# Moving and weight operands of the fp32r matmuls placed at fixed offsets by padding the on-chip pools

## The chip, the cores and the metric

The kernel runs on one core of a Trainium2 chip. The metric is the device time of one execution in microseconds (us). The kernel before took 1050.9 us (median of three runs, 1048.54 to 1056.88).

## The reference, cut to what matters

Two transformer blocks are applied to one sequence of 256 tokens with 1024 features, all in fp32:

- Block one: `x += 0.5*g*swiglu(h)` (hidden width 2816), then a mixer (latent attention with 8 heads beside a short convolution, merged by sigmoid gates and an output projection), then a second swiglu. Each `h` is an RMS norm of `x`, scaled and shifted by vectors that a 1024 x 9216 matrix makes from a condition vector `c`.
- Block two: a mixer of two attentions with gates, a feed-forward `square(relu(h @ w_ff1)) @ w_ff2` (hidden width 4096), a gated addition, and a final RMS norm.

Nearly all of the work is in products of a 256-token activation with weight matrices of 1024 rows or 1024 columns. None of the values computed differ between the two kernels.

## The kernel before

**Three products per tile.** Every fp32 weight tile `raw` that arrives by DMA is split by `split` (L130 to L141) into two fp32r tiles, `hi` (ScalarE, L139) and `lo` (VectorE, L140), and every activation likewise (`hilo`, L171). `mm3` (L149) then issues three matmuls into one PSUM region: `hi` with the high activation, `hi` with the low one, `lo` with the high one:

```
pe.matmul(ps, lhsT=wh, rhs=xh, ...)   # L150
pe.matmul(ps, lhsT=wh, rhs=xl, ...)   # L151
pe.matmul(ps, lhsT=wl, rhs=xh, ...)   # L152
```

`lhsT` is the stationary operand (the weights, 128 x 128, loaded by a LDWEIGHTS), `rhs` is the moving one (128 x 256 tokens). From the loops there are 7,536 fp32r matmuls of 256 columns, and 84 of 384 to 512. In 420 of the 7,620 (latent projection, the heads of both mixers, `natural`) `mm3n` (L166) turns the roles around: there the activation is stationary and the weight tile moves.

**Stages.** In order: the start (condition vector, first norm); swiglu one; mixer one; swiglu two; mixer two; the feed-forward of block two; the gated end. In a swiglu (`swiglu`, `stream_ffn`, 11 iterations) `make` computes 96 matmuls of gate and up strips into the tiles `gu`, and `second` 48 matmuls of the down projection into four accumulators `acc0` to `acc3`, one iteration behind. The feed-forward of block two does the same in 16 iterations, with 48 matmuls into `u` and 48 into `acc`. Other products are in `gl`, `y`, `po` (mixer one) and `qa`, `qkb`, `ya`, `gab`, `po` (mixer two). SyncE issues the weight DMAs; each engine works in program order, and TensorE is fed by the splits of ScalarE and VectorE that run ahead of it.

**Where tiles lie.** In each partition the pools lie one after the other (`const`, `wp`, `tmp`, `res`, then the pools of a stage: `mp` in the streamed feed-forwards, `px` in the mixers), each tile after the one before it, rounded up to 32 bytes. So the size of what comes earlier sets the offset of what follows. In bytes modulo 128, the kernel before has:

| tiles | pool | offset mod 128 |
|---|---|---|
| `hh`, `hl` (activation of most products), `pH`, `pL` | `res` | 0 |
| `mh`, `ml` (activation of the down projections) | `mp` | 0 |
| `ocH`, `ocL`, `mg`, `oAH`, `oAL`, `oBH`, `oBL` | `px` | 0 |
| `oaH`, `oaL`, and `cqH`, `cqL`, `ckH`, `ckL` | `px` of mixer one | 64 |
| `hi`, `lo` of all strips outside the down projections | `wp` | 96 |
| `hi`, `lo` of swiglu one's down projection (`at=(8, 8)`) | `mp`, 2 buffers | 32 and 32, then 96 and 96 |
| the same, swiglu two (`at=(4, 12)`) | `mp` | 16 and 48, then 80 and 112 |
| the same, feed-forward of block two (`at=(8, 4)`) | `mp` | 32 and 16, then 96 and 80 |
| `ident`, `ones1024`, `sq` (moving, plain fp32) | `const`, `tmp` | 32 |

`at` is a pair of offsets in fp32 elements (4 bytes) inside tiles that are 16 elements longer than the 2048 needed; because of these 64 bytes the second of the two buffers lies 64 bytes further on modulo 128. Within a tile, the pieces that matmuls read start at multiples of 512 bytes, so an offset holds for all of them.

Of the kernel before, what the change touches and what calls it, by code (L numbers as in the profile page):

```python
# [8 lines left out]
F32 = mybir.dt.float32  # L9
# [9 lines left out]
P = 128  # L19
# [42 lines left out]
def tile_two_blocks(ctx: ExitStack, tc: tile.TileContext, t: dict, out: bass.AP):  # L62
# [3 lines left out]
    const = ctx.enter_context(tc.tile_pool(name="const", bufs=1))  # L66
    wp = ctx.enter_context(tc.tile_pool(name="wp", bufs=3))
    tmp = ctx.enter_context(tc.tile_pool(name="tmp", bufs=2))
    res = ctx.enter_context(tc.tile_pool(name="res", bufs=1))
# [4 lines left out]
    def bankA(name):  # L74
        return psA.tile([P, 512], F32, tag="acc", name=name)
# [23 lines left out]

    start = tc.tile_pool(name="start", bufs=1)  # L100
    start_ctx, start = start, start.__enter__()
    c_raw = const.tile([P, 8], F32, name="c_raw")
    sync.dma_start(out=c_raw, in_=t["c"][0].rearrange("(p k) -> p k", k=8))
    x_nat = start.tile([P, 2048], F32, name="x_nat")
# [24 lines left out]

    def split(raw, kc, n, wp=wp, bufs=3, at=None):  # L130

        pad = 16 if at else 0
        hi, lo = (wp.tile([P, 2048 + pad], F32R, tag=n_, name=n_, bufs=bufs)[:, o:o + 2048]
                  for n_, o in zip(("hi", "lo"), at or (0, 0)))
        tot = kc * n
        step = tot // pieces[0]
        for s in range(0, tot, step):
            sl = slice(s, s + step)
            act.copy(hi[:, sl], raw[:, sl])  # L139
            vec.tensor_tensor(out=lo[:, sl], in0=raw[:, sl], in1=hi[:, sl].bitcast(F32), op=ALU.subtract)  # L140
        return tuple(z[:, :tot].rearrange("p (k n) -> p k n", k=kc) for z in (hi, lo))  # L141
# [7 lines left out]
    def mm3(ps, wh, wl, xh, xl, start, stop):  # L149
        pe.matmul(ps, lhsT=wh, rhs=xh, start=start, stop=False, skip_group_check=True)  # L150
        pe.matmul(ps, lhsT=wh, rhs=xl, start=False, stop=False, skip_group_check=True)  # L151
        pe.matmul(ps, lhsT=wl, rhs=xh, start=False, stop=stop, skip_group_check=True)  # L152
# [127 lines left out]
    def ada_one(s, which, i):  # L280
        yield from ada_four(s * 24 + which * 8 + i)
        if which == 1:
            ada_scale(s, i, 4)
        if which == 2:
            vec.tensor_scalar_mul(gT[:, s * 8 + i:s * 8 + i + 4], modT[:, s * 24 + 16 + i:s * 24 + 20 + i],
                                  1.0 if s == 1 else 0.5)

    def ada_rest(plan, per, lag=1):

        todo = [ada_one(*a) for a in plan]  # L290
        begun = [[] for _ in range(lag)]
        step = 0
        while todo or any(begun):
            for g in begun.pop(0):
                next(g, None)
            n = per[step % len(per)]
            step += 1
            begun.append(todo[:n])
            todo = todo[n:]
            for g in begun[-1]:  # L300
                next(g)
            yield

    ada_plan = [(s, which, i) for s in range(3) for which in range(3) for i in (0, 4)][4:]

    def drain(g):
        for _ in g:
            pass
# [73 lines left out]
    def stream_ffn(nit, make, w2, finish, extra=None, at=None):  # L382
        with tc.tile_pool(name="mp", bufs=2) as mp:
            ada_tile[:] = [(lambda: mp.tile([P, 2048], F32, tag="ada", name="ada", bufs=2), 4)]
            acc = [bankA(f"acc{i}") for i in range(4)]

            def second(i, mh, ml, w):
                for q in range(4):
                    for d in (2 * q, 2 * q + 1):
                        ps = acc[q][:, (d % 2) * T:(d % 2) * T + T]  # L390
                        for j in range(2):
                            mm3(ps, w[0][:, j, d * P:(d + 1) * P], w[1][:, j, d * P:(d + 1) * P], mh[:, j, :], ml[:, j, :],
                                i == 0 and j == 0 and d % 2 == 0, i == nit - 1 and j == 1)
                    if i == nit - 1:
                        for d in (2 * q, 2 * q + 1):
                            finish(d, acc[q][:, (d % 2) * T:(d % 2) * T + T])

            prev = None
            for i in range(nit):
                mh = mp.tile([P, 2, T], F32R, tag="mh", name="mh")  # L400
                ml = mp.tile([P, 2, T], F32R, tag="ml", name="ml")
                make(i, mh, ml, mp)
                if prev is not None:
                    second(*prev)
                prev = (i, mh, ml, cols(w2, 0, D, 2 * i, 2, at=at, wp=mp, bufs=2))
                if extra is not None:
                    next(extra, None)
            if extra is not None:
                drain(extra)
            second(*prev)  # L410
# [13 lines left out]
    def swiglu(h, w13, w2, gcol, extra=None, fill=None, then=(), first=None, at=None):  # L424
        def make(i, mh, ml, mp):
            if i == 0 and first:
                bb = first
            else:
                g, u = up_strips(w13, i)
                bb = [bankB("gu") for _ in range(2)]  # L430
            if i == 0 and fill is not None:
                fill()
            if i == 0 and not first:
                gemm_many([(b[:, o:o + T], w, j * P) for j, b in enumerate(bb) for o, w in ((0, g), (T, u))], h, KD)
            for j, b in enumerate(bb):
                if i:
                    gemm(b[:, :T], g, j * P, h, KD)
                    gemm(b[:, T:], u, j * P, h, KD)
                s = tmp.tile([P, T], F32, tag="s", name="s")
                m = tmp.tile([P, T], F32, tag="m", name="m")  # L440
                tab(s, b[:, :T], AF.Silu)
                vec.tensor_tensor(out=m, in0=s, in1=b[:, T:], op=ALU.mult)
                hilo(m, mh[:, j, :], ml[:, j, :])
            if i < len(then):
                then[i]()
        stream_ffn(11, make, w2, residual(gcol), extra, at)
# [13 lines left out]
    gt = lambda s: gT[:, s * 8:s * 8 + 8]  # L460
# [82 lines left out]
    h = h_tiles()  # L543

    h = h_tiles()
    rope_steps = rope_table()
# [5 lines left out]
    first = [bankB("gu") for _ in range(2)]  # L552
# [15 lines left out]
    def gemm_half(i):  # L568
# [13 lines left out]
    start_ctx.__exit__(None, None, None)  # L582
    swiglu(h, t["ffn_w13"][0][0], t["ffn_w2"][0][0], gt(0), ada_rest(ada_plan[:8], (0, 0, 1, 1, 1, 1, 1, 1, 1, 1)),
           then=(lambda: None, vector_columns, transpose_p, lambda: next(rope_steps), lambda: None,
                 lambda: drain(rope_steps)), first=first, at=(8, 8))
    mid = ada_rest(ada_plan[8:12], (1,))


    def mixer_one(px, tmp2):
        h = modulated(nw(1), sh(1))  # L590
# [35 lines left out]
        def latent():  # L626
# [19 lines left out]
            for tk in range(2):  # L646
# [2 lines left out]
                vec.tensor_scalar_mul(kr[:, tk, :], bb[tk][:, 384:416], r[:, 3 * tk + 2:3 * tk + 3])  # L649
                rope(kro[:, tk:tk + 1, :], kr[:, tk:tk + 1, :], 1, tk, 1)  # L650
            yield
            cqH = px.tile([P, 2, T], F32R, tag="oaH", name="cqH")
            cqL = px.tile([P, 2, T], F32R, tag="oaL", name="cqL")
            ckH = px.tile([P, T], F32R, name="ckH")
# [254 lines left out]
        return bt  # L909

    h = modulated(nw(2), sh(2))
    swiglu(h, t["ffn_w13"][0][1], t["ffn_w2"][0][1], gt(2), ada_rest(ada_plan[12:], (1,)), fill=bias_rows, at=(4, 12))


    def mixer_two(px, tmp2):
# [290 lines left out]
    h, make_rb = gained("mlp")  # L1206
    rbs = []

    def make(i, mh, ml, mp):
        w = cols(t["w_ff1_2"][0], i * 256, 256)  # L1210
        b = bankB("u")
        for j in range(2):
            gemm(b[:, j * T:(j + 1) * T], w, j * P, h, KD)
        if i == 0:
            rbs.append(make_rb())
        s = mp.tile([P, 2, T], F32, tag="s2", name="s")
        m = mp.tile([P, 2, T], F32, tag="m2", name="m")
        vec.scalar_tensor_tensor(out=s, in0=halves(b), scalar=0.0, in1=rbs[0].unsqueeze(1).to_broadcast([P, 2, T]),
                                 op0=ALU.max, op1=ALU.mult)
        act.activation(m, s, AF.Square)  # L1220
        hilo(m, mh, ml)

    stream_ffn(16, make, t["w_ff2_2"][0], add_x, at=(8, 4))


    with tc.tile_pool(name="px3", bufs=1) as px:
# [4 lines left out]
        h, make_rb = gained("ple")  # L1231
# [7 lines left out]
        def finish(part, c0, n, banks):  # L1239

            for tk in range(2):
                for i in range(n):
                    tr(banks[tk][:, i * P:(i + 1) * P], xT[:, c0 + i, tk * P:(tk + 1) * P])
                fin[part, tk] = banks[tk][:, :n * P]
            for tk in range(2):
                junk = px.tile([P, 512], F32, tag="junk", name="junk", bufs=2)
                act.activation(junk[:, :n * P], fin[part, tk], AF.Square, accum_out=s2[:, tk, part:part + 1])
                sl = slice(c0 * P, (c0 + n) * P)
                if part < 2:
                    vec.tensor_tensor(out=fg[tk][:, sl], in0=fin[part, tk], in1=gbc[:, sl], op=ALU.mult)  # L1250
# [104 lines left out]
```

## Time and profile before

| | |
|---|---|
| time of three runs | 1056.88, 1050.9, 1048.54 us; median 1050.9 us |
| time of the profiled execution | 1048.57 us |
| its span, first to last instruction | 1046.8 us |
| mean granted TensorE clock | 0.995 |
| busy: PE, VectorE, ScalarE, GpSimd | 97%, 71%, 53%, 3% |
| chain of waits: PE, VectorE, ScalarE, DMA | 82%, 9%, 3%, 3% |

Each matmul is recorded with a duration of about 280 ns, which overlaps the next matmuls. What a matmul costs in a dense stream is the distance from its start to the start of the next one; this text calls that a slot. It is read from two rows of the time-ordered list: the last start of a block less the first, divided by the matmuls between them.

### The profile page before, as it was taken

How to read it: one execution, taken by the hardware profiler on the slowest of the kernel's cores; microseconds unless marked ns; L12 is line 12 of the kernel's file. 1: busy time of each engine (PE TensorE's matmuls, PEld its weight loads, DVE VectorE, ACT ScalarE, POOL GpSimd, SP SyncE). 2: the span in 40 equal slices, each digit the busy share in tenths (PEclk: the TensorE clock that was granted, in tenths of full speed). 3: DMA queues.
4: the chain of work that ended last, by engine and by line, in shares of the span. 5: the costliest groups of instructions: out<-in, count | busy, mean ns of one | idle time of the engine just before them, and what ended most of it. 6: DMA issues, size and time to landing. Idle time of an engine off the chain costs nothing.

```text
span 1046.8 us, 20303 instructions
## 1 busy us (share of the span) xinstructions
PE 1018.4 (97%) x8332; PEld 984.3 (94%) x8332; DVE 741.7 (71%) x1414; ACT 557.3 (53%) x1036; POOL 34.9 (3%) x47
## 2 busy tenths in 40 slices
PE   6999999999999999999999999999999999999996
PEld 3799999999989998999999999999899999999996
DVE  4789998657967998964545689656467776555565
ACT  5564554447656455643444555544456665445453
POOL 0000000010000011000000100001100100000010
PEclk9999999999999999999999999999999999999998
DMA  9899999425754987986554344445335885555311
GB/s 346 287 373 337 304 343 367 142 87 173 214 178 151 290 262 271 343 274 212 170 193 153 112 128 155 135 135 165 96 123 188 267 285 186 183 187 195 121 62 41
DMA packets 161301, 215.41 MB, mean 206 GB/s; under 512 B 6206, under 2 KB 129877, under 8 KB 161080
## 3 DMA queue, kind: packets, MB, share of 16 engines
q1 hardware_dynamic: 159346, 212.58, 61.4%
q10 hardware_dynamic: 1862, 1.53, 0.5%
q8 instruction: 65, 1.06, 0.4%
q14 instruction: 28, 0.23, 0.1%
HBM read 210.63 MB, written 3.47 MB: 205 GB/s over the span
## 4 chain that ended last, share of the span: by engine, by line
PE 82%; DVE 9%; ACT 3%; DMA 3%; issue 1%; POOL 0%; SPq 0%; DVEq 0%; ACTq 0%; POOLq 0%
PE gu L150 8%; PE gu L152 8%; PE gu L151 8%; PE acc L150 7%; PE acc L151 7%; PE acc L152 6%; DVE lo L140 3%; PE u L152 2%; PE u L150 2%; PE u L151 2%; PE gab L150 1%; DMA ada<-in_w_ada_dram 1%; ACT hi L139 1%; PE gab L152 1%; PE gab L151 1%
## 5 line engine op out<-in xcount | busy, mean ns | idle before, releaser
L140 DVE TENSOR_TENSOR lo<-raw,hi 128x512 fp32r<-128x512 f32 (+2 forms) x454 | 395.7, 903 | 102.9 <-ACT hi L139 101.7
L139 ACT CAST hi<-raw 128x512 fp32r<-128x512 f32 (+2 forms) x454 | 337.1, 786 | 222.3 <-PE acc L151 81.6
L150 PE MATMUL gu<-hh,hi 128*128 128x256 f32 x704 | 198.8, 283 | 0.0
L152 PE MATMUL gu<-hh,lo 128*128 128x256 f32 x704 | 197.6, 281 | 0.0
L151 PE MATMUL gu<-hl,hi 128*128 128x256 f32 x704 | 196.8, 280 | 0.0
L150 PE MATMUL acc<-mh,hi 128*128 128x256 f32 x608 | 170.2, 282 | 2.3 <-ACT mh L172 2.3
L151 PE MATMUL acc<-ml,hi 128*128 128x256 f32 x608 | 170.8, 281 | 0.0
L152 PE MATMUL acc<-mh,lo 128*128 128x256 f32 x608 | 170.2, 280 | 0.0
L151 PEld LDWEIGHTS gu<-hl,hi 128*128 128x128 f32 x704 | 133.0, 189 | 0.6 <-issue 0.5
L150 PEld LDWEIGHTS gu<-hh,hi 128*128 128x128 f32 x704 | 132.9, 189 | 0.6 <-issue 0.5
L152 PEld LDWEIGHTS gu<-hh,lo 128*128 128x128 f32 x704 | 132.8, 189 | 0.1
L150 PEld LDWEIGHTS acc<-mh,hi 128*128 128x128 f32 x608 | 114.0, 188 | 2.8 <-ACT mh L172 2.8
L151 PEld LDWEIGHTS acc<-ml,hi 128*128 128x128 f32 x608 | 114.5, 188 | 0.2 <-DVE ml L173 0.2
L152 PEld LDWEIGHTS acc<-mh,lo 128*128 128x128 f32 x608 | 114.7, 189 | 0.0
L267 DVE SCALAR_TENSOR_TENSOR ada_acc<-ada,c_act,ada_acc 128x512 f32<-128x512 f32 x98 | 73.6, 751 | 2.3 <-DMA ada<-in_w_ada_dram 0.6
L150 PE MATMUL u<-hh,hi 128*128 128x256 f32 x256 | 71.6, 280 | 0.0
L151 PE MATMUL u<-hl,hi 128*128 128x256 f32 x256 | 71.6, 280 | 0.0
L152 PE MATMUL u<-hh,lo 128*128 128x256 f32 x256 | 71.5, 279 | 0.0
L88 ACT ACTIVATE s<-gu 128x256 f32<-128x256 f32 x44 | 16.7, 382 | 75.2 <-PE gu L152 75.2
L331 POOL TENSOR_TENSOR ssum<-ssum,sq 128x256 f32<-128x256 f32 x25 | 23.3, 931 | 813.6 <-ACT sq L329 812.6
L151 PEld LDWEIGHTS u<-hl,hi 128*128 128x128 f32 x256 | 48.1, 188 | 0.2 <-DVE hl L376 0.2
L150 PEld LDWEIGHTS u<-hh,hi 128*128 128x128 f32 x256 | 48.1, 188 | 0.0
(379 smaller groups left out, 2221.9 us busy)
## 6 DMA issues: line engine op xcount, KB each, us to landing
raw<-in_ffn_w_dram SPq DMA_DIRECT2D x64, 1024.0 KB
raw<-in_w_in_dram SPq DMA_DIRECT2D x37, 1024.0 KB
raw<-in_w_ff_dram SPq DMA_DIRECT2D x32, 1024.0 KB
ada<-in_w_ada_dram SPq DMA_DIRECT2D x28, 1024.0 KB
raw<-in_w_out_dram SPq DMA_DIRECT2D x8, 1024.0 KB
ada<-in_w_ada_dram SPq DMA_DIRECT2D x8, 768.0 KB
raw<-in_w_branch_dram SPq DMA_DIRECT2D x8, 512.0 KB
raw<-in_w_out_a_dram SPq DMA_DIRECT2D x4, 1024.0 KB
```

Source lines behind the costliest of these rows:

```text
L88: last_table[0] = act.activation(*args, **kw).ins
L139: act.copy(hi[:, sl], raw[:, sl])
L140: vec.tensor_tensor(out=lo[:, sl], in0=raw[:, sl], in1=hi[:, sl].bitcast(F32), op=ALU.subtract)
L150: pe.matmul(ps, lhsT=wh, rhs=xh, start=start, stop=False, skip_group_check=True)
L151: pe.matmul(ps, lhsT=wh, rhs=xl, start=False, stop=False, skip_group_check=True)
L152: pe.matmul(ps, lhsT=wl, rhs=xh, start=False, stop=stop, skip_group_check=True)
L267: vec.scalar_tensor_tensor(out=acc, in0=wv[:, k, :], scalar=c_act[:, k0 + k:k0 + k + 1], in1=acc, op0=ALU.mult, op1=ALU.add)
L331: pool.tensor_tensor(out=s[0], in0=s[0], in1=sq, op=ALU.add)
```

## The change

Unused tiles are put into three pools, and the two offsets of the streamed feed-forwards are made equal everywhere.

- `pad_w`, 24 fp32 elements (96 bytes) at the head of `const`, moves everything behind it by 96 bytes: `wp` goes from 96 to 64 modulo 128, `ident`, `ones1024` and `sq` from 32 to 0.
- `pad_x`, 8 elements (32 bytes) at the head of `res`, moves `res` and the stage pools by 128 bytes in all, so their tiles stay at 0.
- `pad_o`, 16 elements (64 bytes) in `px` of mixer one, moves what is created after it: `cqH`, `cqL`, `ckH`, `ckL`, `oaH`, `oaL` from 64 to 0.
- In `split`, tiles with an `at` become 32 elements longer (128 bytes) instead of 16, and all three `at` become (16, 16): `hi` and `lo` of the down projections lie at 64 modulo 128 in both buffers.

No instruction is added, removed or reordered.

```
+    const.tile([P, 24], F32, name="pad_w")
+    res.tile([P, 8], F32, name="pad_x")
     c_raw = const.tile([P, 8], F32, name="c_raw")
...
-        pad = 16 if at else 0
+        pad = 32 if at else 0
...
-                 lambda: drain(rope_steps)), first=first, at=(8, 8))
+                 lambda: drain(rope_steps)), first=first, at=(16, 16))
...
+            px.tile([P, 16], F32, name="pad_o")
             cqH = px.tile([P, 2, T], F32R, tag="oaH", name="cqH")
...
-    swiglu(h, ..., fill=bias_rows, at=(4, 12))
+    swiglu(h, ..., fill=bias_rows, at=(16, 16))
...
-    stream_ffn(16, make, t["w_ff2_2"][0], add_x, at=(8, 4))
+    stream_ffn(16, make, t["w_ff2_2"][0], add_x, at=(16, 16))
```

## Rows read from the trace of the kernel before

**Rows 1.** The page, busy time: busy us, share of the span, instructions

```profile
PE 1018.4 (97%) x8332; PEld 984.3 (94%) x8332; DVE 741.7 (71%) x1414; ACT 557.3 (53%) x1036; POOL 34.9 (3%) x47
```

**Rows 2.** Stretches: length; busy per engine; granted clock; DMA share; GB/s

```profile
35.90:225.50 189.60, 189.60 (x1676) 188.77 (x1675) 159.32 (x250) 100.01 (x147) 2.26 (x4) 1.00 0.84 287
```

**Rows 3.** The page, costliest groups: line, operation, count, busy us, mean ns

```profile
L150 PE MATMUL gu<-hh,hi 128*128 128x256 f32 x704 | 198.8, 283 | 0.0
...
L150 PE MATMUL acc<-mh,hi 128*128 128x256 f32 x608 | 170.2, 282 | 2.3 <-ACT mh L172 2.3
...
L150 PE MATMUL u<-hh,hi 128*128 128x256 f32 x256 | 71.6, 280 | 0.0
```

**Rows 4.** List in order of time: start us, duration us; a `gu` block, 95 slots

```profile
80.78 0.28 PE L150 MATMUL gu<-hh,hi 128*128 128x256 f32 x1
...
91.86 0.28 PE L152 MATMUL gu<-hh,lo 128*128 128x256 f32 x1
```

**Rows 5.** The same list, a later `gu` block from its second matmul, 94 slots

```profile
98.17 0.28 PE L151 MATMUL gu<-hl,hi 128*128 128x256 f32 x1
...
109.24 0.28 PE L152 MATMUL gu<-hh,lo 128*128 128x256 f32 x1
```

**Rows 6.** The same list, down projection of swiglu one, 47 slots

```profile
91.98 0.28 PE L150 MATMUL acc<-mh,hi 128*128 128x256 f32 x1
...
97.54 0.28 PE L152 MATMUL acc<-mh,lo 128*128 128x256 f32 x1
```

**Rows 7.** The same list, swiglu two, both buffers, 47 slots each

```profile
500.39 0.28 PE L150 MATMUL acc<-mh,hi 128*128 128x256 f32 x1
...
505.92 0.28 PE L152 MATMUL acc<-mh,lo 128*128 128x256 f32 x1
...
517.25 0.28 PE L150 MATMUL acc<-mh,hi 128*128 128x256 f32 x1
...
522.79 0.28 PE L152 MATMUL acc<-mh,lo 128*128 128x256 f32 x1
```

**Rows 8.** The same list, feed-forward of block two, both buffers, 47 slots each

```profile
863.24 0.28 PE L150 MATMUL acc<-mh,hi 128*128 128x256 f32 x1
...
868.82 0.28 PE L152 MATMUL acc<-mh,lo 128*128 128x256 f32 x1
...
874.54 0.28 PE L150 MATMUL acc<-mh,hi 128*128 128x256 f32 x1
...
880.09 0.28 PE L152 MATMUL acc<-mh,lo 128*128 128x256 f32 x1
```

**Rows 9.** The same list, a `y` block of mixer one, 47 slots

```profile
350.66 0.28 PE L150 MATMUL y<-ocH,hi 128*128 128x256 f32 x1
...
356.25 0.28 PE L152 MATMUL y<-oaH,lo 128*128 128x256 f32 x1
```

**Rows 10.** The same list, `qa` of mixer two (weights moving), 63 slots

```profile
610.43 0.28 PE L168 MATMUL qa<-lo,hh 128*128 128x256 f32 x1
...
617.88 0.28 PE L168 MATMUL qa<-lo,hh 128*128 128x256 f32 x1
```

**Rows 11.** Plain fp32 matmuls: ns min/median/max of `bs`; two merged rows of the list

```profile
L1006 PE MATMUL bs<-kA,qA x4: 379/379/382, 642.3 to 643.0; 128*128 128x256 f32 x4
...
642.31 1.03 PE L1006 MATMUL bs<-kA,qA 128*128 128x256 f32 x4
...
1017.39 1.03 PE L340 MATMUL nrm_ps<-sq,ones 128*128 128x256 f32 x4
```

**Rows 12.** Line L140 in two stretches: ns min/median/max, first and last start

```profile
L140 DVE TENSOR_TENSOR lo<-raw,hi x44: 1018/1220/1228, 98.9 to 217.5; 128x1024 fp32r<-128x1024 f32 x40, 128x832 fp32r<-128x832 f32 x4
...
L140 DVE TENSOR_TENSOR lo<-raw,hi x57: 683/1220/1227, 448.8 to 589.2; 128x1024 fp32r<-128x1024 f32 x45, 128x512 fp32r<-128x512 f32 x12
```

**Rows 13.** Chain of waits between 330 and 400: start us, us, what

```profile
345.71 7.35 DMA raw<-in_w_in_dram
...
394.75 4.49 DVE lo L140 x3
```

More of the change, by code (lines that the diff above doesn't have):

```diff
@@ L911, in tile_two_blocks @@
     h = modulated(nw(2), sh(2))
-    swiglu(h, t["ffn_w13"][0][1], t["ffn_w2"][0][1], gt(2), ada_rest(ada_plan[12:], (1,)), fill=bias_rows, at=(4, 12))
+    swiglu(h, t["ffn_w13"][0][1], t["ffn_w2"][0][1], gt(2), ada_rest(ada_plan[12:], (1,)), fill=bias_rows, at=(16, 16))
     def mixer_two(px, tmp2):
```

## The prediction

> **What bounds the kernel now.** I read the page's busy times first: PE is busy 97% of the span, 8,332 matmuls, while VectorE, the next, stands at 71% [rows 1]. [...] So neither a wait nor the clock is the limit, but the length of a slot. The costliest groups say where the slots are: `gu` 704 matmuls on each of three lines, `acc` 608, `u` 256 [rows 3]; with the rest of the loops 7,536 of 256 columns. Their recorded 280 ns overlap, so they say nothing of the slot, and I went to the list in order of time for it.
>
> [...]
> - `gu`, moving at 0 and weights at 96: 11.08/95 = 116.6 ns in one block [rows 4], 11.07/94 = 117.8 in another [rows 5]. Of the 34 blocks of `gu` and `u` after the first, worked out alike, 25 are of the short form and 9 of the long one, none in between, so it is a locked rhythm and not noise.
> - `acc`, moving at 0: 5.56/47 = 118.3 with weights at 32 [rows 6]; 117.7 and 117.9 at 16/48 and 80/112 [rows 7]; 118.7 and 118.1 at 32/16 and 96/80 [rows 8].
> - `y`: 118.9 over a block [rows 9], half of it with moving at 0 and half with moving at 64, weights at 96. If the first half runs at 117.4, the middle of the two `gu` forms, the second half runs at 120.4.
> - `qa`, moving (here the weights) at 96, stationary at 0: 118.25 [rows 10].
>
> **The change part by part.** It adds no instruction, wait or transfer, and moves none past another. It moves addresses, so its whole price is (slots) x (change of the slot). No row of before has fp32r weights at 64 with moving at 0, so the new slot is unknown and I bound it. [...] Above by 120.4 ns, the slowest pairing seen [rows 9]; worse is not excluded, but has no row. Between these I take 116.7, the short form of `gu`: it is the nearest row (moving at 0, the same matmul, weights 32 bytes off, in every buffer alike), and in the rows weights at one common offset in both buffers and both parts are found in `gu` alone.
> - Strips in `wp` (`gu`, `u`, `gl`, `qkb`, `ya`, `gab`, `po`, `pg` and small ones), 96 to 64: 5,280 slots, now (25 x 116.7 + 9 x 117.8)/34 = 117.0. At 116.7: 5,280 x 0.3 = 1.6 us less.
> - Down projections, to 64 in both buffers: 528 slots at 118.3, 528 at 117.8, 768 at 118.4, in the mean 118.2. At 116.7: 1,824 x 1.5 = 2.7 us less.
> - `oaH`, `oaL` from 64 to 0: 96 slots from 120.4 to 116.7: 0.4 us less.
> - Products with the weights moving, 96 to 64: 336 slots from 118.25 to 116.7 would be 0.5 us less; the 84 wider ones at the same 1.5 ns are 0.1. This term I trust least, as moving does not come to 0 there, whatever the words of the change say; I count 0.3.
> - Plain fp32 operands from 32 to 0: nothing. `kA` moves at 0 and `sq` at 32, and both take 1.03 us for four [rows 11].
> - Splits: VectorE's 1,024-column subtraction has the same median, 1220 ns, and the same ceiling, 1227 and 1228, with destinations at 32 and 96 as with 16, 48, 80 and 112 [rows 12]. I cost it at nothing, and a few ns on each would hide under PE. Weight loads overlap PE (PEld 94% busy, [rows 1]) and are inside the slot as measured.
> - Landing of `raw` at 64 instead of 96 in `wp`: no row separates it. Only a wait of PE would show it, and the chain has few: 7.35 us of DMA at 345.7 [rows 13]. A tenth on that either way is 0.7 us; I take 0.
> - What comes back: between 345 and 399 us the chain runs through DMA and VectorE's splits [rows 13], so shorter slots of `gl` and `y` only lengthen waits for `lo`. That is about a tenth of the slots: 0.3 us of the gain is lost, and next late there is the split, not PE.
>
> Sum: 1.6 + 2.7 + 0.4 + 0.3 - 0.3 = 4.7 us, some 5, off the profiled execution's 1048.57 (span 1046.8 and 1.8 around it): 1043.9. That execution lies 2.3 us under the median of the three runs and agrees with the lowest, so I forecast **1044 us**, 0.7% under the median. One percent, 10.5 us, is about what a measurement of this kernel tells from no change; over 7,536 slots that is 1.4 ns a slot. The mean slot is now (5,280 x 117.0 + 1,824 x 118.2 + 96 x 120.4 + 336 x 118.25)/7,536 = 117.4; the line lies at 116.0 and at 118.8.
>
> [...] The rows at moving 0 differ by 2 ns with the weights' address alone [rows 4, 7, 8]. [...]
>
> **Rivals.**
> 1. *Nothing in the mean: it trades.* `gu` has 96 already, and 25 of 34 blocks there run the short form; another offset may lock them more often into the long one, while `acc` gains. If all settle at 117.5, between the short and the long form, `wp` loses 5,280 x 0.5 = 2.6 us and `acc` wins 1,824 x 0.7 = 1.3: 1050. [...] For it: `acc` at 96/96 in swiglu one is not at 116.7 although `gu` at 96 is, so the offset modulo 128 is not all that counts. Chance 0.26.
> 2. *Below anything seen.* [...] Chance 0.22.
> 3. *Slower.* [...] Place: every strip of `wp`. Price: 5,280 x 3.4 + 1,824 x 2.2 = 22 us, less the tenth that hides behind splits: 1068. It decides from a mean of 118.8 on. Against: of the pairings with moving at 0 none is over 118.7. Chance 0.16.
>
> **How the numbers follow.** The forecast, all near 116.7, has 0.36. Faster by over 1% (under 1040.4): rival 2 and a lower tail of the forecast, 0.22 + 0.04 = 0.26. Slower by over 1% (over 1061.4): rival 3, 0.16. Within: 0.32 + 0.26 = 0.58. The range takes the forecast's own spread (1038 to 1048) and rival 1 whole, half of rival 2 down to 1031, and rival 3 only up to 1060, its mild form (mean slot 118.9): about 0.2 is left out.
>
> **What would show it.** In the time-ordered list of the changed kernel the same blocks: `gu` at 116.6 or 116.7 in all 34 blocks, with the 117.8 form gone; `acc` the same in both buffers of all three stages; `y` without a difference between its halves; `qa` near 117 to 118; plain fp32 at 217, the 1,024-column subtraction at 1220. PE's busy time should fall by some 5 us and its idle time stay. Wrong would be: `acc` still above 117.5 (then the offset modulo 128 is not what sets it), `gu` above 118 (rival 3) or under 115.5 (rival 2), or a gain in slots that comes back as waits for `lo` before 400 us.

## The result, and the profile after

The changed kernel took 1039.7 us (median of four runs, 1037.9 to 1044.1), the kernel before 1053.7 beside it; the ratio is 0.990, 95% interval 0.987 to 0.993. The kernel before spread from 1048.5 to 1056.9 us there, so the quotient of the two medians, 0.987, overstates the gain; its later medians, over sets of 7 to 25 runs, were 1049.0 to 1049.6, and on these 1039.7 is 0.991. The profiled execution took 1041.2 us (span 1039.4) against 1048.6 (span 1046.8). The time lies inside the predicted range, 4 us under the forecast of 1044. What the slots did inside it was not what the forecast said.

The page after, for [rows 1] (in the changed file the three matmul lines are L152 to L154):

```profile
PE 1010.6 (97%) x8332; PEld 976.3 (94%) x8332; DVE 741.4 (71%) x1414; ACT 557.1 (54%) x1036; POOL 35.0 (3%) x47
```

The stretch of swiglu one, columns as in [rows 2]:

```profile
35.65:224.60 188.95, 188.95 (x1677) 188.30 (x1675) 159.22 (x250) 99.41 (x146) 2.21 (x3) 1.00 0.83 287
```

PE's busy time fell by 7.8 us (1018.4 to 1010.6) and the span by 7.4; VectorE and ScalarE are where they were, and the granted clock in swiglu one is 1.00 as before. So the gain is in the slots, which only the list in order of time shows.

A `gu` block and an `acc` block of swiglu one, for [rows 4 to 6]: start, duration, first and last matmul.

```profile
97.52 0.28 PE L153 MATMUL gu<-hl,hi 128*128 128x256 f32 x1
...
108.59 0.28 PE L154 MATMUL gu<-hh,lo 128*128 128x256 f32 x1
108.71 0.28 PE L152 MATMUL acc<-mh,hi 128*128 128x256 f32 x1
...
114.24 0.28 PE L154 MATMUL acc<-mh,lo 128*128 128x256 f32 x1
```

`gu`: 11.07/94 = 117.8 ns; `acc`: 5.53/47 = 117.7. The same two in swiglu two, for [rows 7]:

```profile
507.02 0.28 PE L152 MATMUL gu<-hh,hi 128*128 128x256 f32 x1
...
517.78 0.28 PE L154 MATMUL gu<-hh,lo 128*128 128x256 f32 x1
517.90 0.28 PE L152 MATMUL acc<-mh,hi 128*128 128x256 f32 x1
...
523.22 0.28 PE L154 MATMUL acc<-mh,lo 128*128 128x256 f32 x1
```

Here it is 10.76/95 = 113.3 and 5.32/47 = 113.2: the same addresses, the same instructions, 4.5 ns less. In the whole trace the unbroken stretches of strips and down projections have just two rhythms: a **short** one of 113, 113, 114 ns (mean 113.3), and a **long** one of 117 to 119 (mean 117.8). The 116.7 of the kernel before [rows 4] is gone. Once in a rhythm, PE stays in it until something interrupts it, or until it slips. The slip of swiglu two, at the border from `gu` to `acc`:

```profile
501.34 0.28 PE L153 MATMUL gu<-hl,hi 128*128 128x256 f32 x1
501.46 0.28 PE L154 MATMUL gu<-hh,lo 128*128 128x256 f32 x1
501.58 0.28 PE L152 MATMUL acc<-mh,hi 128*128 128x256 f32 x1
501.69 0.28 PE L153 MATMUL acc<-ml,hi 128*128 128x256 f32 x1
```

Up to 501.46 the slots are of the long form, from 501.58 on of the short one, which lasts to 594 us. Swiglu one is nearly all long: its small bias products (`ada_ps`) come between every two iterations, and the first slot after them, 201 or 202 ns, leads into the long rhythm each time. The feed-forward of block two starts long and is short from 842 us to its end at 1002, for [rows 8]. In all, 1,379 of 5,134 strip slots (27%) and 1,147 of 1,815 slots of the down projections (63%) stand in short stretches (three neighbours of at most 114 ns). `y` and `qa`, for [rows 9, 10], run long too in the blocks shown before: 5.53/47 = 117.7 and 7.42/63 = 117.8:

```profile
349.99 0.28 PE L152 MATMUL y<-ocH,hi 128*128 128x256 f32 x1
...
355.52 0.28 PE L154 MATMUL y<-oaH,lo 128*128 128x256 f32 x1
...
608.57 0.28 PE L170 MATMUL qa<-lo,hh 128*128 128x256 f32 x1
...
615.99 0.28 PE L170 MATMUL qa<-lo,hh 128*128 128x256 f32 x1
```

What should not move did not, for [rows 11, 12]: four plain fp32 records in a row, with `sq` moved from 32 to 0, take 1.03 us as before, (1.03 - 0.38)/3 = 217 ns each when the last one's 0.38 is taken off, and the subtraction's median is 1218 ns (min/median/max below).

```profile
1010.16 1.03 PE L342 MATMUL nrm_ps<-sq,ones 128*128 128x256 f32 x4
...
L142 DVE TENSOR_TENSOR lo<-raw,hi x44: 1019/1218/1227, 98.2 to 216.7; 128x1024 fp32r<-128x1024 f32 x40, 128x832 fp32r<-128x832 f32 x4
```

### The profile page after: what moved, and what is told of

It is laid out like the page before. It is cut to its first block, busy times and chain, and to the rows that moved or that the text cites. A ratio compares the mean times of both kernels' runs of the same rounds, so it can differ in the third digit from the quotient of the medians.

```text
span 1039.4 us, 20303 instructions
## 1 busy us (share of the span) xinstructions
PE 1010.6 (97%) x8332; PEld 976.3 (94%) x8332; DVE 741.4 (71%) x1414; ACT 557.1 (54%) x1036; POOL 35.0 (3%) x47
## 4 chain that ended last, share of the span: by engine, by line
PE 84%; DVE 9%; ACT 3%; DMA 2%; issue 1%; POOL 0%; ACTq 0%; DVEq 0%; POOLq 0%; SPq 0%
PE gu L152 8%; PE gu L153 8%; PE gu L154 8%; PE acc L152 6%; PE acc L153 6%; PE acc L154 6%; DVE lo L142 3%; PE u L154 2%; PE u L153 2%; PE u L152 2%; PE gab L152 2%; PE gab L154 1%; PE gab L153 1%; ACT hi L141 1%; PE gl L153 1%
## 5 line engine op out<-in xcount | busy, mean ns | idle before, releaser
L152 PE MATMUL gu<-hh,hi 128*128 128x256 f32 x704 | 198.1, 282 | 0.0
L154 PE MATMUL gu<-hh,lo 128*128 128x256 f32 x704 | 196.7, 280 | 0.0
L152 PE MATMUL acc<-mh,hi 128*128 128x256 f32 x608 | 168.3, 278 | 2.3 <-ACT mh L174 2.3
L153 PE MATMUL acc<-ml,hi 128*128 128x256 f32 x608 | 168.6, 278 | 0.0
L154 PE MATMUL acc<-mh,lo 128*128 128x256 f32 x608 | 168.4, 277 | 0.0
L152 PEld LDWEIGHTS gu<-hh,hi 128*128 128x128 f32 x704 | 132.8, 189 | 0.7 <-issue 0.5
L154 PEld LDWEIGHTS gu<-hh,lo 128*128 128x128 f32 x704 | 132.9, 189 | 0.2 <-DVE lo L142 0.2
L152 PEld LDWEIGHTS acc<-mh,hi 128*128 128x128 f32 x608 | 114.0, 188 | 2.7 <-ACT mh L174 2.7
L154 PEld LDWEIGHTS acc<-mh,lo 128*128 128x128 f32 x608 | 114.2, 188 | 0.0
L152 PE MATMUL u<-hh,hi 128*128 128x256 f32 x256 | 71.0, 277 | 0.0
L154 PE MATMUL u<-hh,lo 128*128 128x256 f32 x256 | 70.8, 277 | 0.0
L152 PEld LDWEIGHTS u<-hh,hi 128*128 128x128 f32 x256 | 48.1, 188 | 0.0
```

## The experiments

Two theories stood at the start. **T1:** the offset of the weights modulo 128 sets the slot, at 64 a shorter rhythm exists, and which rhythm a stretch gets is a matter of how it starts and what it runs beside. **T2**, the rival: the gain is the down projections' alone, or that of equal offsets in both buffers, and the strips only trade. For all kernels the mean slot was worked out from the same list: the start-to-start distances under 135 ns of 256-column matmuls, in strips (with their moving operand at 0) and in the down projections. Slots are those of the one profiled execution, times the median of all; for `e2_strips_only` that execution took 1056.5 us, 4.6 above its median.

| kernel | strips | down proj. | time, us | ratio to before (95%) |
|---|---|---|---|---|
| before | 117.1 | 118.2 | | 1 |
| after | 116.6 | 115.0 | 1039.7 | 0.990 (0.987 to 0.993) |
| `e1_down_only` | 117.2 | 117.1 | 1046.3 | 0.997 (0.996 to 0.998) |
| `e2_strips_only` | 117.7 | 118.4 | 1051.9 | 1.003 (1.001 to 1.004) |
| `e3_weights_0` | 118.8 | 119.3 | 1057.3 | 1.008 (1.006 to 1.010) |
| `e4_down_96` | 117.0 | 117.4 | 1047.4 | 0.998 (0.997 to 0.999) |
| `e9_all_64_stride` | 114.9 | 114.2 | 1037.2 | 0.988 (0.986 to 0.991) |
| `e10_moving_256` | 116.6 | 114.9 | 1039.5 | 0.990 (0.988 to 0.992) |
| `e11_hi64_lo192` | 113.8 | 113.4 | 1029.5 | 0.981 (0.978 to 0.983) |
| `e12_hi192_lo64` | 117.2 | 118.5 | 1048.6 | 0.999 (0.996 to 1.002) |

**One part alone, down projections.** The kernel before with

```
-        pad = 16 if at else 0          # three calls: at=(8, 8), (4, 12), (8, 4)
+        pad = 32 if at else 0          # three calls: at=(16, 16)
```

> Down projections alone to 64 (the at and the 32-element pad), strips stay at 96, no pads in the pools. Locked-rhythm theory (with moving at 0 and weights at 64 the stream of matmuls falls into one of two rhythms, 113.3 or 117.8 ns a slot, and keeps it until something interrupts it): acc blocks at 113.3 or 117.8, gu and u at 116.7 or 117.8 as before, and the rhythm is chosen anew at every border between acc and gu, so at most 1,824 x 4.9 = 9 us of gain, 1044 to 1050. Rival, the down projections' offsets were all that was wrong: the whole gain, ratio to before 0.990.

Measured: 0.3% faster. Two neighbouring `acc` blocks of swiglu one, in the two buffers:

```profile
91.55 0.28 PE L150 MATMUL acc<-mh,hi 128*128 128x256 f32 x1
...
96.89 0.28 PE L152 MATMUL acc<-mh,lo 128*128 128x256 f32 x1
...
108.72 0.29 PE L150 MATMUL acc<-mh,hi 128*128 128x256 f32 x1
...
114.27 0.28 PE L152 MATMUL acc<-mh,lo 128*128 128x256 f32 x1
```

5.34/47 = 113.6 and 5.55/47 = 118.1: the short rhythm is there with the strips still at 96, but it ends with its block, since the strips beside it run at 116.7 or 117.8; in swiglu two, and in the last feed-forward but for its first block, `acc` stayed long.

**The other part alone, strips and pads.** The changed kernel with `pad = 16` and the three old `at`.

> Pads in the pools alone (strips at 64, oaH at 0), down projections as before at 32/96, 16/48 and 32/16. Locked-rhythm theory: gu and u in 113.3 or 117.8, acc as before at 117.7 to 118.8; short gu and u blocks fewer than in the changed kernel, since acc at other offsets interrupts the rhythm 22 times and 32 times; ratio to before 0.993 to 1.002. Rival, the strips carry the gain: ratio 0.990.

Measured: 0.3% slower, at the upper end of the first expectation. A `gu` block:

```profile
97.59 0.28 PE L153 MATMUL gu<-hl,hi 128*128 128x256 f32 x1
...
108.67 0.28 PE L154 MATMUL gu<-hh,lo 128*128 128x256 f32 x1
```

11.08/94 = 117.9, and so nearly everywhere: alone, 64 costs the strips the 116.7 form and gives them next to nothing. The parts sum to nothing, the whole gives 1%: the gain is an interaction. As the traces read, the short rhythm needs strips and down projections that both allow it, so that it carries over the borders.

**Another offset for all.** The changed kernel with `pad_w` of 8 elements, `pad_x` of 24 and `at=(0, 0)`: weights and moving both at 0.

> All weights at 0 modulo 128 instead of 64, moving at 0 as in the changed kernel (pads of 8 and 24 elements, at of 0 and 0). If what helps is that both operands start on multiples of 64 bytes, 0 is as good as 64: slots of 113.3 and 117.8 and the time of the changed kernel, ratio 0.990. If what helps is that the two reads start half of 128 bytes apart, 0 is the worst offset: slots over 118, ratio 1.005 to 1.03.

Measured: 0.8% slower; a whole `acc` block has 5.64/47 = 120.0 ns. So the value counts, not that all are alike, and a common multiple of 64 bytes is not enough: the second expectation came out.

```profile
91.92 0.28 PE L152 MATMUL acc<-mh,hi 128*128 128x256 f32 x1
...
97.56 0.28 PE L154 MATMUL acc<-mh,lo 128*128 128x256 f32 x1
```

**Equal offsets at 96.** The kernel before with `pad = 32` and `at=(24, 24)` three times.

> The kernel before with all weights of the down projections at 96 in both buffers and both parts, as its strips are. If one common offset is what counts (the forecast's reason for 116.7), acc comes to 116.7 or 117.8 from 118.2: 1 to 3 us less than before, ratio 0.997. If 64 is what counts, acc stays at 118 and the time is that of before, and no slot of 113.3 is seen for a whole block. Either way no 113.3 rhythm.

Measured: 0.2% faster. `acc` in its two buffers, 5.58/47 = 118.7 and 5.48/47 = 116.6; no stretch of this kernel keeps 113.3. T2's "equal offsets alone" gives a fifth of the gain, and at 96 the short rhythm was not seen.

```profile
161.22 0.28 PE L150 MATMUL acc<-mh,hi 128*128 128x256 f32 x1
...
166.80 0.28 PE L152 MATMUL acc<-mh,lo 128*128 128x256 f32 x1
...
178.52 0.28 PE L150 MATMUL acc<-mh,hi 128*128 128x256 f32 x1
...
184.00 0.28 PE L152 MATMUL acc<-mh,lo 128*128 128x256 f32 x1
```

**Can a start be steered?** Extra matmuls of 256 and then 24 i columns ahead of the `gu` blocks 1 to 10, 16 i columns ahead of the `u` blocks; their values are overwritten.

```
+        if i:
+            kick(bb[0], g, h, 256, 24 * i)     # u blocks: kick(b, w, h, 16 * i)
```

> The changed kernel with short extra matmuls ahead of each streamed block, whose result the block's own first matmul overwrites: in the two swiglus one of 256 columns and one of 24 x i columns (i = 1 to 10), in the feed-forward of block two one of 16 x i columns (i = 1 to 15). The output is the same. Locked-rhythm theory: the extra slot shifts the phase, so some lengths put gu or u into the 113.3 rhythm for the whole block and others into 117.8, the same length doing the same in both swiglus; no third rhythm. Rival, the rhythm belongs to the stage (its tiles, its DMA load) and not to the phase: swiglu one stays at 117.8 for every length and the feed-forward at 113.3. Time a few us over the changed kernel from 35 extra blocks of 0.2 to 0.4 us.

Measured: 1054.9 us, one run, 15 over the changed kernel where a few were expected: the mean slots are 117.7 in strips and 116.0 in down projections. Of the 35 blocks that started anew 34 entered the long rhythm, whatever the length of the kick; some slipped to the short one at the border to `acc`, without an order in the lengths. The block with i = 3 in swiglu one, 11.07/94 = 117.8, and the `acc` behind it, 5.34/47 = 113.6:

```profile
80.36 0.28 PE L153 MATMUL gu<-hl,hi 128*128 128x256 f32 x1
...
91.43 0.28 PE L154 MATMUL gu<-hh,lo 128*128 128x256 f32 x1
91.55 0.28 PE L152 MATMUL acc<-mh,hi 128*128 128x256 f32 x1
...
96.89 0.28 PE L154 MATMUL acc<-mh,lo 128*128 128x256 f32 x1
```

So neither expectation held. The rhythm does not belong to the stage: in the last feed-forward, short in the changed kernel, the interrupted blocks were long. The length of a matmul ahead is no handle on it.

**The changed kernel once more**, unedited.

> The changed kernel once more, for a second trace. Locked-rhythm theory: again every block at 113.3 or 117.8 and nothing between; blocks that restart after fp32 or bf16 matmuls with a slot of 201 ns are at 117.8 again; where the stream slips into 113.3 may differ from the first trace, which is where the spread of 1037.9 to 1044.1 us comes from. Rival, the rhythm follows the stage alone: the same blocks as in the first trace.

Measured: 1041.4 us; again long after every bias product of swiglu one, but the slip of swiglu two came 32 us earlier, at 469 instead of 501:

```profile
468.96 0.28 PE L154 MATMUL gu<-hh,lo 128*128 128x256 f32 x1
469.08 0.28 PE L152 MATMUL acc<-mh,hi 128*128 128x256 f32 x1
469.19 0.28 PE L153 MATMUL acc<-ml,hi 128*128 128x256 f32 x1
```

That is 32 us at 4% less a slot, 1.2 us of the time. When it slips differs from run to run. The changed kernel's runs spread over 6.2 us, but not by that alone: the slowest, 1044.1, also has the lowest mean granted clock, 0.989 against 0.995; the other three spread over 3.4.

Where it slips has an order that the lengths of the kicks do not show. The two buffers of a down projection lie at 64 and at 192 modulo 256, `hi` and `lo` alike, and the strips at 192; the moving tiles `hh`, `hl`, `mh` and `ml` lie at 0 (worked out from the sizes of the tiles). In the traces of the changed kernel, of this repeat, of `e5_kick_map` and of `e10_moving_256` below, `acc` was entered 72 times from the long rhythm without a pause: within ten slots 20 of the 39 blocks in the buffer at 64 were short, and none of the 33 in the buffer at 192. So the strips at 192 keep the short rhythm but seldom start it, and in `e2_strips_only` no down projection at 64 starts it for them; that this is the whole of the interaction is argued from these counts, not shown by a run of its own.

**Neighbours of 64.** Strips and down projections of one stage at an offset of its own: 60, 56 and 72 in one kernel, 48, 80 and 68 in the other. The strips' `hi` and `lo` tiles become 2,080 elements long for it, with the weights inside (`where[0]` is set per stage), the pads are 8 and 24 elements, and a scratch tile of the start has one buffer instead of two.

```
-        hi, lo = (wp.tile([P, 2048 + pad], ...)[:, o:o + 2048] ... at or (0, 0)))
+        hi, lo = (wp.tile([P, 2080], ...)[:, o:o + 2048] ... at or (where[0], where[0])))
```

> The kernel after, with the strips and the down projections of one stage at one common offset of its own: 60 bytes in swiglu one, 56 in swiglu two, 72 in the last down projection (moving at 0 throughout, the rest at 64). Theory A (64 is special, since it cuts the line of 128 bytes in half or starts a piece of 64): no slot of 113.3 ns in any of the three stages, gu and acc between 116.5 and 118.5, and the run gives back what the change won: 1046 to 1052 us. Theory B (the offset sets a delay between the two reads, and the short rhythm has a width round 64): 113.3 or a form within 1 ns of it at 60 or 72 too, and if 60 or 72 has no long form beside it, gu there is near 113.3 in all blocks: swiglu one 4 ns x 900 slots = 3.5 us less than in the kernel after.

> As the run before it, with 48 bytes in swiglu one, 80 in swiglu two and 68 in the last down projection. Theory A: no slot of 113.3 ns anywhere in the three stages, 116.5 to 118.5 instead. Theory B: 68 shows 113.3 as 64 does, 48 and 80 forms between those of 64 (113.3 and 117.8) and of 32 and 96 (116.7 and 117.8).

Measured: 1060.3 and 1058.6, one run each, and no stretch that keeps 113.3 in the six stages: `gu` at 56, shown, has 11.25/95 = 118.4; `u` at 68 has 117.9 to 118.9, at 72 117.8 to 120.0 from the second block on. Theory A holds: four bytes off 64 the short rhythm is gone. The first time missed its range by 8 us, for another reason. The strip and `acc` means are those of the kernel before; but from the last `po` of mixer one to the first `gu` of swiglu two it took 14.7 us instead of 7.8, and between 402 and 418 us PE's granted clock stood at 0.75 and 0.50 of full, after a wait for VectorE's splits (4.47 us of the chain, from 400.34); the second fence is a stretch of it, columns as in [rows 2]. The kernel before has 0.79 and 1.00 in the same two stretches. It is not these kernels' own: the profiled execution of `e2_strips_only` has 0.53 and 0.61 there. One run of each shows that it happened, not how often.

```profile
500.05 0.28 PE L152 MATMUL gu<-hh,hi 128*128 128x256 f32 x1
...
511.30 0.28 PE L154 MATMUL gu<-hh,lo 128*128 128x256 f32 x1
```

```profile
410.00:418.00 8.00, 8.00 (x28) 6.00 (x27) 4.45 (x10) 5.31 (x11) 0.00 (x0) 0.50 0.54 203
```

The surprise was beside the point of these two: their strips outside the three stages, at 64 as in the changed kernel, ran mostly short (`po` at 113.6 and 113.5 in the mean, 117.8 in the changed kernel). Modulo 128 nothing differed; above it, the longer tiles had moved the buffers, and the pads the moving operands.

**Above 128 bytes.** All at 64, with the 2,080-element tiles everywhere; and, to part the two differences, the changed kernel with `pad_x` of 72 elements instead of 8.

> All weights of strips and down projections at 64 and moving at 0 modulo 128, as in the kernel after, but each hi and lo tile of the strips is 8,320 bytes long instead of 8,192 (the weights sit 64 bytes inside it), so hi and lo and the three buffers no longer lie at one offset modulo 512 (448 for all before; now 448/320, 192/64, 64/448), and moving lies at 0 instead of 256 modulo 512. In the two runs before this one the strips outside the streams had this layout: gl, po and gab ran mostly at 113.3 ns after the same 200 to 202 ns restarts that lead to 117.8 in the kernel after, and their long form was 118.9. Theory A1 (modulo 128 alone decides which rhythms exist, and which is entered is chance): as the kernel after, strips near 116.6, 1038 to 1044 us. Theory A2 (the layout above 128 bytes decides which rhythm is entered and kept: with unlike offsets of hi and lo the long rhythm doesn't hold): gu, u and acc fall into 113.3 within some 30 slots of each restart and stay: strips in the mean near 114, acc near 113.5, (116.6 - 114) x 5,280 + (115 - 113.5) x 1,824 = 16 us less than the kernel after: 1020 to 1030 us.

> The kernel after with one pad 256 bytes longer: the moving operands at 0 instead of 256 modulo 512 and the down projections' weights at 64/320 and 192/448, strips at 448 for hi and lo as in the kernel after. It separates the two differences of the run before: if it is where moving lies modulo 512, gl, po, gab and gu run mostly at 113.3 here too (1020 to 1032 us); if it is the unlike offsets of hi and lo, the strips stay mostly at 117.8 as in the kernel after (1037 to 1044 us). Theory A1 expects 1037 to 1044 as well.

Measured: with the longer tiles strips at 114.9 and 1037.2 us (1036.1 to 1041.6), which lies between the ranges of A1 and A2 and does not part in time from the changed kernel's 1037.9 to 1044.1; with the moving operands shifted by 256 (and the down projections' tiles with them), all as in the changed kernel. So what shortens the slots is where `hi` and `lo` lie. The list shows it slot by slot. From 115.9 us the weights have `hi` at 192 and `lo` at 64 modulo 256, and the slots are of a long form, 118.9 over a whole block; from 118.65 on `hi` lies at 64 and `lo` at 192:

```profile
118.53 0.28 PE L154 MATMUL gu<-hh,lo 128*128 128x256 f32 x1
118.65 0.28 PE L152 MATMUL gu<-hh,hi 128*128 128x256 f32 x1
...
119.25 0.28 PE L154 MATMUL gu<-hh,lo 128*128 128x256 f32 x1
119.36 0.28 PE L152 MATMUL gu<-hh,hi 128*128 128x256 f32 x1
...
119.70 0.28 PE L152 MATMUL gu<-hh,hi 128*128 128x256 f32 x1
```

118.53 to 119.25 is 0.72/6 = 120 a slot, 119.36 to 119.70 is 0.34/3 = 113.3, and so it stays to the end of the `acc` block behind it, at 132 us.

**The two orders.** In every buffer of strips and down projections `hi` at 64 and `lo` at 192 modulo 256, or the other way round; modulo 128 both are the changed kernel.

```
+    wp.tile([P, 32], F32, tag="pad_hi", ...)      # e11; none in e12
     hi = [wp.tile([P, 2048], F32R, tag="hi", ...) ...]
+    wp.tile([P, 32], F32, tag="pad_lo", ...)
     lo = [wp.tile([P, 2048], F32R, tag="lo", ...) ...]
...                                                # the down projections' pool likewise
-    at=(16, 16)
+    at=(16, 32)                                   # pads of 16 and 32 elements; e12: 48 and 32, pad_x 40
```

> The kernel after, with hi at 64 and lo at 192 modulo 256 in every buffer of the strips and the down projections (a pad of 128 bytes before hi and one between hi and lo; modulo 128 everything is as in the kernel after, moving at 0 modulo 256 as there). In the run with the longer tiles the time-ordered list of gu shows what sets the rhythm: at 119.3 us the first weights with hi at 64 and lo at 192 modulo 256 turn the long rhythm into 113.3 within six slots, and a block that starts on such weights after a 201 ns restart is at 113.3 from its second slot; with hi at 192 and lo at 64 the long rhythm stays (118.9), with hi and lo alike (the kernel after) also (117.8). Theory B1 (the order 64/192 modulo 256 makes the short rhythm the only one that lasts): all strips and all acc at 113.3 to 113.6, that is (116.6 - 113.5) x 5,134 + (115.0 - 113.4) x 1,815 = 18.8 us off the profiled 1041.2 of the kernel after, less 3 to 6 that come back as waits before 400 us and at the start: 1024 to 1030 us. Theory B2 (chance, or the change of layout from buffer to buffer did it): strips 115 to 117.8, 1034 to 1042 us.

> The same with the two offsets exchanged: hi at 192, lo at 64 modulo 256 in every buffer, everything still at 64 and moving at 0 modulo 128. Theory B1: the long rhythm of 118.9 after every restart and no way out of it; strips 118.5 to 119, acc the same: (118.8 - 116.6) x 5,134 + (118.8 - 115) x 1,815 = 18 us over the kernel after, 1055 to 1062 us, slower than the kernel before though all operands stand where the change wants them modulo 128. Theory B2: 1034 to 1044 us.

Measured: 1029.5 us (1028.5 to 1030.1), 1.9% under the kernel before, and 1048.6 (1043.3 to 1056.5), no different from it. The first, its busy time on the page:

```profile
PE 996.7 (97%) x8332; PEld 960.5 (93%) x8332; DVE 740.8 (72%) x1414; ACT 557.3 (54%) x1036; POOL 35.1 (3%) x47
```

Its `gu` block that answers to the one of swiglu one above, after the same restart:

```profile
98.05 0.28 PE L160 MATMUL gu<-hl,hi 128*128 128x256 f32 x1
...
108.71 0.28 PE L161 MATMUL gu<-hh,lo 128*128 128x256 f32 x1
```

10.66/94 = 113.4, and so in all blocks of swiglu one from here on, where the changed kernel had 117.8. The second:

```profile
97.01 0.28 PE L160 MATMUL gu<-hl,hi 128*128 128x256 f32 x1
...
108.18 0.28 PE L161 MATMUL gu<-hh,lo 128*128 128x256 f32 x1
...
74.85 0.28 PE L160 MATMUL acc<-ml,hi 128*128 128x256 f32 x1
...
80.06 0.28 PE L161 MATMUL acc<-mh,lo 128*128 128x256 f32 x1
```

11.17/94 = 118.8 in the one, 5.21/46 = 113.3 in the other, an earlier block. B1 is right on the order 64/192: only the short rhythm lasts in strips and down projections. On 192/64 it was wrong by half: the long rhythm lasts there, but so does the short one where a stretch enters it, as 28% of the strip slots did, and the expected 1055 to 1062 did not come. `e11_hi64_lo192` is the fastest kernel of this study, beats both kernels and has the narrowest runs (1.7 us between the extremes of four, 13 us between those of ten of its mirror image).

**From where the order counts.** The two kernels hold one more test, in `y` of mixer one: it uses weights of one layout with two sorts of moving tiles in turn. `ocH` and `ocL` lie at 0; `oaH` and `oaL`, which `pad_o` puts at a multiple of 128, lie at 128 modulo 256 (again from the sizes of the tiles). First the kernel with `hi` at 64 and `lo` at 192, then its mirror image:

```profile
347.66 0.28 PE L159 MATMUL y<-ocH,hi 128*128 128x256 f32 x1
...
349.03 0.28 PE L159 MATMUL y<-oaH,hi 128*128 128x256 f32 x1
...
350.33 0.28 PE L161 MATMUL y<-oaH,lo 128*128 128x256 f32 x1
```

```profile
335.60 0.28 PE L159 MATMUL y<-ocH,hi 128*128 128x256 f32 x1
...
337.02 0.28 PE L159 MATMUL y<-oaH,hi 128*128 128x256 f32 x1
...
338.28 0.28 PE L161 MATMUL y<-oaH,lo 128*128 128x256 f32 x1
```

With `hi` at 64, `oc` takes 1.37/12 = 114.2 and `oa` 1.30/11 = 118.2; with `hi` at 192, `oc` takes 1.42/12 = 118.3 and `oa` 1.26/11 = 114.5, and so in all 13 unbroken pieces of twelve in each trace. So the order counts from the moving tile: short where `hi` lies 64 bytes beyond it and `lo` 192, modulo 256, and long in these pieces the other way round. Which tile it is does not matter, since the two kernels exchange the roles. The short `acc` blocks of `e1_down_only` fit: its moving tiles lie at 128, and all of them are in the buffer at 192.

## Why the prediction was right, and where not

**What bounds it: right.** The slot is the limit. PE's idle time (span less busy) went from 28.4 to 28.8 us, and 7.8 of its busy time came off.

**The new slot: the step that failed.** "I take 116.7, the short form of `gu`": no unbroken block of strips or down projections in the changed kernel has it. The upper bound of 120.4 held; no run shows how short a slot can be, and the shortest rhythm measured is 113.3. The value is two values, 113.3 and 117.8, and a mean of them is no rhythm. The choice came from the nearest row, with weights 32 bytes off; four bytes off are too far. The offsets were also counted modulo 128 alone: modulo 256 the moving tiles of `gu` and `acc` lay at 128 in the kernel before and at 0 after, and by the runs above it is the distance of the weights from them, modulo 256, that tells the rhythms apart.

**The terms.** Strips: predicted 1.6 us less, measured 5,134 x (117.07 - 116.59) = 2.5. That their mean, 116.6, stands beside the 116.7 of the forecast is luck: 27% of the slots are short and most of the others long, and the share depends on when the stream slips. Down projections: 2.7 predicted, 1,815 x (118.22 - 114.98) = 5.9 measured; this is the mis-sized term. `oaH` and `oaL`: 0.4 predicted, 96 x (119.84 - 116.72) = 0.3. Weights moving: 0.3 predicted, 322 x (118.34 - 117.14) = 0.4. All fp32r slots, waits among them, went from 927.6 to 919.3 us, and the span fell by 7.4: some 0.9 came back, where 0.3 was predicted. Fp32 and splits, costed at nothing, were nothing. Against the median of 1050.9 from which the chances were counted, 1039.7 is just inside "faster by over 1%", which had 0.26.

**The rivals.** Two came true at once, in different stretches, and cancelled by half. Rival 1 said that 64 may lock strips "more often into the long one, while `acc` gains": 73% of the strip slots are outside the short rhythm, at 117.8 where 25 of 34 blocks were at 116.7, and `e2_strips_only` alone is slower. Rival 2, a slot under 115.5, came in the short stretches, 3.4 ns under 116.7. No run shows the terms from which its chance of 0.22 and the 1031 of the range were counted; in their place the runs showed 113.3 ns in the short stretches and, with all of them short, the 1029.5 us of `e11_hi64_lo192`. A multiple of 64 is not enough for it: weights at 0 are the worst of all (118.8 and 119.3). Rival 3, slower, has its case in `e3_weights_0`, 1057.3 us, at 0 and not at 64; no run shows a reason for the 0.16 that it had at 64.

**The weights' place alone.** With the same instructions and the same loads beside them the slot goes from 113.3 to 120.0 ns with nothing but the weights' place (`e11_hi64_lo192` and `e3_weights_0`, moving at 0 modulo 256 in both). By the two halves of `y`, 114.2 and 118.2 ns on one layout of weights, what counts is how the loaded weight tile and the moving one lie to each other; so far as the slot goes the two are not independent in this kernel.

**What stays open.** Why 64, and why `hi` 64 beyond the moving tile with `lo` 192 beyond it makes the long rhythm decay and the other orders do not. No run moves the moving tiles by 128 with all weights kept; the halves of `y` are the only place where both positions stand beside one layout of weights, and `e10_moving_256` only says that a shift by 256 does nothing. Of `e11_hi64_lo192`'s gain in slots over the changed kernel, 919.3 - 905.2 = 14.1 us, the span shows 11.5; its first `gu` starts 1.5 us later, which two traces of the changed kernel do by 2.1 from one to the other.

## What to carry to other kernels

Where PE is busy all the time, list the start-to-start distances of its matmuls before looking for waits, and give each rhythm its own count; a mean over blocks hides two. Where the operands' addresses can be moved by a pad, try offsets over 256 bytes, not 128, counted from the moving operand, for all streams that alternate on the engine together, since one stream alone gained 0.3% or lost as much and both together 1.0%, with the order of `hi` and `lo` 1.9%. A kernel that slips between two rhythms can have a wide spread (13 us between the extremes of ten runs of `e12_hi192_lo64`), and one run of it may miss by some us.

## What the runs showed of the hardware that was not expected

- An fp32r matmul of 256 columns has slots of 113.3, 116.7, 117.8, 118.9 or 120.0 ns here, in executions with a mean granted clock of 0.993 to 0.995, by the place of its operands and by the rhythm that its stretch is in; the rhythm, once taken, can last over hundreds of slots (1,427 in one stretch of `e11_hi64_lo192`, 831 to 993 us without a slot over 135 ns: mean 113.3).
- Which of two rhythms a stretch takes differs from run to run with the same program (a slip at 469 us or at 501).
- What counts is where the weights lie from the moving tile, modulo 256: in `y` weights of one layout give 114 ns with one moving tile and 118 with another 128 bytes off, in both mirror kernels.
- In swiglu one the first slot after the small bias products is 200 to 202 ns in the changed kernel and in `e11_hi64_lo192`; with `hi` at 64 and `lo` at 192 the slots are short from the third on, with `hi` and `lo` alike they are long.
